# Hybrid decoder layer on one core: activation forms of the second MLP product emitted one step earlier, with other first places for banks, row tiles and split tiles

## The chip, the cores and the metric

The kernel runs on one NeuronCore of one Trainium2 chip. The metric is device microseconds of one execution. Before the change the median of three runs is 2827.7 us (2827.36 to 2830.01).

## The reference

One layer of a decoder trunk, for a prompt of 2048 rows and 8 x 8 sample rows, 2112 rows of 1024 columns in all. A token mixer (three head groups behind one input projection, one output projection) comes first, then a squared-ReLU MLP:

```
x = x + rms_norm(mix, norm_mix_post)
h = rms_norm(x, norm_mlp_pre)
f = square(relu(h @ w_mlp_up)) @ w_mlp_down      # 1024 -> 4096 -> 1024
x = x + rms_norm(f, norm_mlp_post)
```

The outputs are x for prompt and sample rows and the new caches and states. The change lies in the MLP alone. Everything is float32.

## The kernel before, in words

**Three passes for one product.** A float32 product is made of three matmuls on operands that are split into a rounded high part (`hi`) and the rest (`lo`): hi x lo, hi x hi, lo x hi (`mm3`, line 282). Splitting a tile costs one cast on ScalarE (ACT) and one subtraction on VectorE (DVE) or GpSimd (POOL). An activation tile (128x352) is split in `s_pair` (line 1608): `shi` is cast on ACT, `slo` subtracted on DVE. A weight tile (128x1024) is split in `w_split` (line 1599): `whi` on ACT, `wlo` on POOL while the first MLP product runs ("up", kind u), on DVE while the second runs ("down", kind d).

**The MLP's tiling.** The rows go in three blocks of 704, each of two halves of 352. In each block both products, up and down, are made by seven part products each (a Strassen scheme: sums and differences of operand quarters are formed, and seven products in place of eight are combined). The orders are 1, 2, 6, 7, 5, 3, 4 for up and 1, 2, 7, 4, 5, 6, 3 for down. A part product is 8 steps; a step takes one weight tile pair. So the list `steps` has 3 x 2 x 7 x 8 = 336 entries. An up step is 24 matmuls of 352 columns into two PSUM banks, each of which is evicted at once by `up_out`. A down step takes two activation tiles, j and j+1 (its two halves), with 9 matmuls of 512 columns each; three banks are filled over the 8 steps and evicted by `down_out` after the last, with 3 additions on DVE for products 1, 2, 7, 4 and 3 (for product 1 copies on ACT), 6 for product 5 and 9 for product 6.

**The forms.** The left operand of down products 7, 5, 6 and 3 is first formed from two activation tiles by one DVE operation per tile (`down_form`, line 1750); products 1, 2 and 4 take a tile as it is. `down_split` (line 1745) makes form and split of one tile; the form is tied behind the DVE instruction that was emitted last before it. The left operand of an up product is four tile pairs, split once per product by `up_split` (line 1740).

**What sets the order.** The loop over `steps` emits the program. A scheduler then orders each engine's instructions: where several could go, the one that was emitted first goes first. The engines run what stands there strictly in order. In the loop each turn emits, one after the other: the load of a weight tile four steps ahead; `w_split` of the next step's weights; near the end of an up product the split of the first two pairs of the next (line 1859); the matmuls of this step and its evictions; the other two pairs (line 1886); and last the forms and splits of the next step, where that is a down step (line 1894).

**Places.** `NSP` (line 49) is the number of buffers for split activation tiles, two per pair. `bank()` (line 1680) hands out PSUM banks in the order psS, psD, psD; its counter starts at 0 and is raised first, so the first bank comes from psD, a pool that opens when the output projection's own PSUM pool closes. Rows of a half (`Half.rows`, line 1616 on) are read back from the scratch tensor `xn_d` into three tiles before they are turned by PE transposes (`pq<-cst,xt`). For the second half they are taken in turn from two tags of a pool shared with the output projection (`XT`, line 1685: xres, x2t).

Of the kernel before, what the change touches and what calls it, by code (L numbers as in the profile page):

```python
# [45 lines left out]
NSUM = 16  # L46
SUM_US = 6.4
SUM_END = {5: "a13", 7: "a13", 6: "a2", 4: "a4"}
NSP = 12

NKEY = 1288

# [92 lines left out]
def hybrid_layer(ctx: ExitStack, tc: tile.TileContext, I, O, stage=9):  # L145
# [83 lines left out]
    def sb(name, bufs, side=None):  # L229
        return tc.tile_pool(name=name, bufs=bufs, side=side, reuse_waits="tile")  # L230
# [15 lines left out]
    def stream(gen, delay=0.0):  # L246
        streams.append([gen, PE.us + delay])
# [1321 lines left out]
    UP_ORDER, DOWN_ORDER = (1, 2, 6, 7, 5, 3, 4), (1, 2, 7, 4, 5, 6, 3)  # L1569
# [24 lines left out]
    def idle_y(at):  # L1594

        kind, _, i, _ = steps[at]
        return kind == "u" and i != UP_ORDER[0]
# [10 lines left out]
    def s_pair(src):  # L1608

        hi = s4.tile([P, HT], F32R, name="shi", tag="s")  # L1610
        lo = s4.tile([P, HT], F32R, name="slo", tag="s")
        A.copy(hi, src)  # L1612
        V.tensor_sub(lo, src, hi.bitcast(F32))
        return hi, lo
# [28 lines left out]
    halves = {}  # L1643
    up_s = {}

    def mlp_ahead():
        nonlocal e4, s4, w4, r4
        psm.close()
        e4 = p4.enter_context(sb("ev4", 2, "right"))
        s4 = p4.enter_context(sb("s4", NSP, "right"))  # L1650
        r4 = p4.enter_context(sb("r4", 8, "right"))
# [18 lines left out]
    y4 = p4.enter_context(sb("y4", 6, "left"))  # L1670
# [4 lines left out]

    V.tensor_scalar(g4[:, 512:], g4[:, 512:], -1.0, None, op0=ALU.mult)

    nbank = [0]

    def bank():  # L1680
        nbank[0] += 1
# [3 lines left out]
    XT = [(epool, "xres"), (epool, "x2t")]  # L1685
# [36 lines left out]
    def up_sums(b):  # L1722

        (q11, q12), (q21, q22) = halves[b, 0].q, halves[b, 1].q
        while len(up_s.get((b, 2), [])) < 4:
            yield 1.0
        s3 = []
        for c in range(4):
            s3.append(f4.tile([P, HT], F32, name="s3", tag="f"))
            with tc.issue_after(V.last):  # L1730
                V.tensor_sub(s3[c], q11[c], q21[c])
                V.tensor_sub(q21[c], q21[c], q22[c])
                V.tensor_sub(q11[c], q21[c], q11[c])
                V.scalar_tensor_tensor(q12[c], q12[c], -1.0, q11[c], op0=ALU.mult, op1=ALU.subtract)
            yield 3.0
        src.update({(b, 6): q11, (b, 7): s3, (b, 5): q21, (b, 3): q12, (b, 4): q22})
# [3 lines left out]
    def up_split(b, i, cs):  # L1740
        up_s.setdefault((b, i), []).extend(s_pair(src[b, i][c]) for c in cs)
# [3 lines left out]
    def down_split(b, i, j):  # L1745
        with tc.issue_after(V.last):
            a = down_form(i, j)
        down_s[b, i, j] = s_pair(a)

    def down_form(i, j):  # L1750
        x = {k[:2]: v for k, v in X.items() if k[2] == j}
        if i == 1:
            a = x[1, 1]
        elif i == 2:
            a = x[1, 2]
        elif i == 7:
            a = t4.tile([P, HT], F32, name="d3", tag="t")
            V.tensor_sub(a, x[1, 1], x[2, 1])
        elif i == 4:
            a = x[2, 2]  # L1760
        elif i == 5:
            a = x[2, 1]
            V.tensor_sub(a, a, x[2, 2])
        elif i == 6:
            a = x[1, 1]
            V.tensor_sub(a, x[2, 1], a)
        else:
            a = x[1, 2]
            V.scalar_tensor_tensor(a, a, -1.0, x[1, 1], op0=ALU.mult, op1=ALU.subtract)
        return a  # L1770

    def down_out(i, p, ps):
        n = TP[p][1]
        ps = ps[:n]

        def y(t, d, new=False):
            if new:
                Y[t, p] = y4.tile([P, D], F32, name=f"y{t}", tag="y")
            return Y[t, p][:n, 512 * (d - 1):512 * d]

        if i == 1:
            A.copy(y(1, 2, True), ps)
        elif i == 2:
            V.tensor_add(y(1, 1), ps, y(1, 2))
        elif i == 7:
            V.tensor_add(y(2, 2, True), ps, y(1, 2))
        elif i == 4:
            V.tensor_add(y(2, 1), ps, y(2, 2))
        elif i == 5:
            for d in ((2, 2), (1, 2)):  # L1790
                V.tensor_sub(y(*d), y(*d), ps)
        elif i == 6:
            for d in ((2, 1), (2, 2), (1, 2)):
                V.tensor_add(y(*d), ps, y(*d))
        else:
            V.tensor_add(y(1, 2), ps, y(1, 2))
# [28 lines left out]

    def second_half(b):

        h = halves[b, 1] = Half(b, 1, XT)
        h.rows()
        yield 10.0  # L1830
        yield from h.turn(psT, "tr")
        yield from up_sums(b)
# [12 lines left out]
    for at, (kind, b, i, jj) in enumerate(steps):  # L1845
        if at + 4 < len(steps):
            w_load(at + 4)
        while nsplit[0] < len(steps) and nsplit[0] <= at + (2 if idle_y(nsplit[0]) else 1):
            w_split(nsplit[0])
            nsplit[0] += 1  # L1850
        order = UP_ORDER if kind == "u" else DOWN_ORDER
        nxt = steps[at + 2] if at + 2 < len(steps) else None

        if kind == "u" and jj == NJ // 2 - 2 and i != UP_ORDER[-1]:
            ni = UP_ORDER[UP_ORDER.index(i) + 1]
            if ni == 6:
                while (b, 6) not in src:
                    advance(min(streams, key=lambda st: st[1]))
            up_split(b, ni, (0, 1))
        if kind == "d" and i == DOWN_ORDER[-1] and jj == NJ // 2 - 1 and (b + 1, 1) in src:  # L1860
            up_split(b + 1, 1, (0, 1))
        two = steps[at + 1] if at + 1 < len(steps) else None
        if kind == "u":
            hi, lo = wts.pop(at)
            s = up_s[b, i]
            for j2 in range(2):
                ps = bank()
                for c in range(4):
                    ws = slice(2 * P * c + P * j2, 2 * P * c + P * j2 + P)
                    mm3(ps[:, :HT], hi[:, ws], lo[:, ws], *s[c], c == 0, c == 3)  # L1870
                up_out(i, 2 * jj + j2, ps)
        else:
            hi, lo = wts.pop(at)
            if jj == 0:
                banks = [bank() for _ in TP]
            for j2 in range(2):
                j = 2 * jj + j2
                s = down_s.pop((b, i, j))
                ws = slice(512 * j2, 512 * j2 + 512)
                for p, (a, n) in enumerate(TP):  # L1880
                    mm3(banks[p][:n], s[0][:, a:a + n], s[1][:, a:a + n], hi[:, ws], lo[:, ws], j == 0, j == NJ - 1)
            if jj == NJ // 2 - 1:
                for p in range(len(TP)):
                    down_out(i, p, banks[p])
        if kind == "u" and jj == NJ // 2 - 1 and i != UP_ORDER[-1]:
            up_split(b, UP_ORDER[UP_ORDER.index(i) + 1], (2, 3))
        if kind == "d" and i == DOWN_ORDER[-1] and jj == NJ // 2 - 1 and b + 1 < TT // BT:
            while (b + 1, 1) not in src:
                advance(min(streams, key=lambda st: st[1]))
            have = len(up_s.get((b + 1, 1), []))  # L1890
            up_split(b + 1, 1, range(have, 4))
        if two is not None and two[0] == "d":
            for j2 in range(2):
                down_split(two[1], two[2], 2 * two[3] + j2)
        if kind == "d":
            end, last = jj == NJ // 2 - 1, b == TT // BT - 1
            if i == 2 and end:
                for p in range(len(TP)):
                    square(1, p, 1)
                    if last:  # L1900
                        o = Y[1, p][:TP[p][1], :512]
                        V.tensor_mul(o, o, g4[:TP[p][1], :512])
            if i == 6 and end:
                for p in range(len(TP)):
                    for d in (1, 2):
                        square(2, p, d)
            if i == 3 and not end and 1 <= jj <= len(TP):
                mlp_out(b, 2, jj - 1)
            if i == 3 and end:
                for p in range(len(TP)):  # L1910
                    square(1, p, 2)
                    mlp_out(b, 1, p, last)
        if kind == "d" and i == 6 and jj == 2 and b + 1 < TT // BT:
            stream(next_block(b + 1))
        if at % 20 == 10 and shifts:
            nm, sr, sb_ = shifts.pop(0)
            with tc.issue_after(wload[0].ins):
                SP.dma_start(O[nm][0, sb_, 0:WB - NS].rearrange("t h e -> t (h e)"),
                                  I[sr][0, sb_, NS:WB].rearrange("t h e -> t (h e)"))
        poll()  # L1920
# [38 lines left out]
```

## Time and profile before

| | us |
|---|---|
| median of three runs | 2827.7 |
| profiled execution, its own time | 2828.42 |
| its span, first to last instruction | 2826.6 |
| PE busy (matmuls) | 2595.9, 92% |
| DVE busy | 1536.4, 54% |
| ACT busy | 1325.4, 47% |
| POOL busy | 1076.7, 38% |
| mean granted TensorE clock | 0.963 |

The first matmul of the MLP (`pm`) starts 1307.5 us into the span, the last at 2809.5 us. Block 0's down products run from 1581.1 to 1836.2 us, block 1's from 2066.9 to 2324.4, block 2's from 2554.4 on. In the trace an idle time stands in brackets behind the instruction that ended it, with what released it. A weight load for matmuls (LDWEIGHTS) is listed as PEld. Where a helper records an operation, its line is the helper's: every DVE and POOL operation of the MLP stands under L137, every matmul under L118, every transpose under L122; L1604 is `whi`, L1612 `shi`, L1638 the turned rows.

### The profile page before, as it was taken

To read this page: it belongs to the slowest core of one execution; us is meant where nothing else is said; L and a number is where in the kernel's file an instruction comes from. 1 tells how busy PE (TensorE), PEld (TensorE's weight loads), DVE (VectorE), ACT (ScalarE), POOL (GpSimd) and SP (SyncE) were. 2 spreads that over 40 slices of the span, in tenths; PEclk is the share of its full clock that TensorE was granted. 3 is DMA by queue.
4 is the path that set the end of the run, shared out by engine and by line. 5 is a ranking of instruction groups with operands and counts; after the bars stand their busy time and mean duration, and the time that the engine had idled before them with its cause. 6 is when DMAs were issued, how large, how long until landed. Compare 5 with 4: busy or idle time off the path is not lost. (4 is left out here: it accounts for less than half of the span.)

```text
span 2826.6 us, 40785 instructions
## 1 busy us (share of the span) xinstructions
PE 2595.9 (92%) x14329; PEld 2194.3 (78%) x14329; DVE 1536.4 (54%) x2994; ACT 1325.4 (47%) x2776; POOL 1076.7 (38%) x1008
## 2 busy tenths in 40 slices
PE   7998889999989978999899999999999998999996
PEld 6897767877877755556899876799987678998764
DVE  4555436455446556454255466744446674445666
ACT  4534335435435333334437644453854355385433
POOL 4445445444454543334566200166610026660002
PEclk9999989999999989999999999999999999999998
DMA  7777998777677559877877445474434446544343
GB/s 207 214 185 223 270 252 230 197 215 206 178 214 205 148 165 285 264 225 245 247 227 206 127 149 162 154 220 135 164 126 147 139 143 195 169 157 134 134 127 86
DMA packets 426261, 528.27 MB, mean 187 GB/s; under 512 B 65482, under 2 KB 326130, under 8 KB 421448
## 3 DMA queue, kind: packets, MB, share of 16 engines
q1 hardware_dynamic: 411352, 483.45, 54.0%
q0 software_dynamic: 14704, 42.21, 9.0%
q8 instruction: 113, 1.85, 0.3%
q14 instruction: 92, 0.75, 0.1%
HBM read 447.90 MB, written 178.19 MB: 221 GB/s over the span
## 5 line engine op out<-in xcount | busy, mean ns | idle before, releaser
L137 POOL TENSOR_TENSOR wlo<-wraw,whi 128x512 fp32r<-128x512 f32 (+2 forms) x359 | 670.8, 1898 | 557.0 <-ACT whi L417 290.6
L1604 ACT CAST whi<-wraw 128x1024 fp32r<-128x1024 f32 x336 | 351.7, 1049 | 360.1 <-PE pm L118 300.8
L118 PE MATMUL pm<-slo,whi 128*128 128x352 f32 x1344 | 439.1, 328 | 15.0 <-DVE slo L137 5.1
L118 PE MATMUL pm<-wlo,shi 128*128 128x512 f32 (+1 forms) x1008 | 404.6, 401 | 42.5 <-ACT shi L1612 41.9
L118 PE MATMUL pm<-shi,whi 128*128 128x352 f32 x1344 | 437.4, 326 | 0.0
L118 PE MATMUL pm<-shi,wlo 128*128 128x352 f32 x1344 | 429.5, 328 | 6.2 <-POOL wlo L137 6.1
L118 PE MATMUL pm<-whi,shi 128*128 128x512 f32 (+1 forms) x1008 | 402.3, 399 | 0.0
L118 PE MATMUL pm<-whi,slo 128*128 128x512 f32 (+1 forms) x1008 | 338.3, 398 | 0.6 <-DVE slo L137 0.6
L137 DVE TENSOR_TENSOR wlo<-wraw,whi 128x1024 fp32r<-128x1024 f32 (+1 forms) x169 | 206.2, 1220 | 204.3 <-ACT whi L1604 200.1
L118 PE MATMUL pj<-lo,whi 128*128 128x512 f32 (+1 forms) x720 | 273.2, 380 | 16.8 <-ACT xr L631 8.5
L118 PEld LDWEIGHTS pm<-slo,whi 128*128 128x128 f32 x1344 | 256.0, 191 | 19.3 <-ACT whi L1604 6.3
L118 PE MATMUL pj<-hi,whi 128*128 128x512 f32 (+1 forms) x720 | 263.5, 366 | 0.0
L118 PEld LDWEIGHTS pm<-wlo,shi 128*128 128x128 f32 (+1 forms) x1008 | 183.5, 182 | 102.7 <-ACT shi L1612 48.6
L118 PE MATMUL pj<-hi,wlo 128*128 128x512 f32 (+1 forms) x720 | 262.9, 366 | 0.0
L137 POOL TENSOR_TENSOR ssf<-ssf 128x1 f32<-128x1 f32 (+1 forms) x18 | 6.7, 373 | 668.1 <-ACT jkf L1805 668.0
L118 PEld LDWEIGHTS pm<-shi,wlo 128*128 128x128 f32 x1344 | 254.8, 191 | 7.5 <-POOL wlo L137 7.4
L118 PEld LDWEIGHTS pm<-shi,whi 128*128 128x128 f32 x1344 | 256.0, 190 | 0.1
L137 DVE TENSOR_TENSOR x<-pm,x 128x352 f32<-128x352 f32 x240 | 124.2, 521 | 222.6 <-PE pm L118 222.4
L118 PEld LDWEIGHTS pm<-whi,slo 128*128 128x128 f32 (+1 forms) x1008 | 182.1, 182 | 55.3 <-DVE slo L137 2.7
L118 PEld LDWEIGHTS pm<-whi,shi 128*128 128x128 f32 (+1 forms) x1008 | 183.9, 182 | 52.6
L1612 ACT CAST shi<-x 128x352 fp32r<-128x352 f32 x288 | 136.8, 484 | 173.7 <-DVE x L137 119.1
L137 DVE TENSOR_TENSOR slo<-x,shi 128x352 fp32r<-128x352 f32 x288 | 157.0, 554 | 40.8 <-ACT shi L1612 38.6
(324 smaller groups left out, 4892.8 us busy)
## 6 DMA issues: line engine op xcount, KB each, us to landing
wraw<-in_w_in SPq DMA_DIRECT2D x192, 256.0 KB
wraw<-u_d SPq DMA_DIRECT2D x96, 512.0 KB
wraw<-d_d SPq DMA_DIRECT2D x96, 512.0 KB
wraw<-in_w_mlp_up SPq DMA_DIRECT2D x72, 512.0 KB
wraw<-in_w_mlp_down SPq DMA_DIRECT2D x72, 512.0 KB
u_d<-in_w_mlp_up POOLq DMA_DIRECT2D x64, 256.0 KB, 5.7
d_d<-in_w_mlp_down POOLq DMA_DIRECT2D x64, 256.0 KB, 7.0
out_s_k<-in_cache_attn_k SPq DMA_DIRECT2D x8, 2040.0 KB
```

Of the source, the lines that this page charges most:

```text
L118: return self.eng.matmul(out, lhsT, rhs, **kw)
L137: out = f(*args, **kw)
L1604: A.copy(hi, raw)
L1612: A.copy(hi, src)
```

## The change

Five edits, all in the MLP's driver.

- Where a down step follows a down step, its forms and splits are emitted ahead of the current step's matmuls and evictions. Where a down step follows an up step, they still come behind the matmuls.
- Three of the four pairs of the next up product are split ahead of the last step but one, and one behind the last, in place of two and two.
- `NSP` is 14 in place of 12.
- The bank counter starts at 2, so the first bank is one of psS.
- The rows of the second half of block 0 go to the pool `y4`, made for the down outputs, in place of `XT`.

```diff
-NSP = 12
+NSP = 14
...
-    nbank = [0]
+    nbank = [2]
...
-        h = halves[b, 1] = Half(b, 1, XT)
+        h = halves[b, 1] = Half(b, 1, XT if b else [(y4, "y")])
...
-            up_split(b, ni, (0, 1))
+            up_split(b, ni, (0, 1, 2))
         if kind == "d" and i == DOWN_ORDER[-1] and jj == NJ // 2 - 1 and (b + 1, 1) in src:
-            up_split(b + 1, 1, (0, 1))
+            up_split(b + 1, 1, (0, 1, 2))
+
         two = steps[at + 1] if at + 1 < len(steps) else None
+        if two is not None and two[0] == "d" and kind == "d":
+            for j2 in range(2):
+                down_split(two[1], two[2], 2 * two[3] + j2)
...
+        if two is not None and two[0] == "d" and kind == "u":
+            for j2 in range(2):
+                down_split(two[1], two[2], 2 * two[3] + j2)
         if kind == "u" and jj == NJ // 2 - 1 and i != UP_ORDER[-1]:
-            up_split(b, UP_ORDER[UP_ORDER.index(i) + 1], (2, 3))
+            up_split(b, UP_ORDER[UP_ORDER.index(i) + 1], (3,))
...
-        if two is not None and two[0] == "d":
-            for j2 in range(2):
-                down_split(two[1], two[2], 2 * two[3] + j2)
```

What this does to the engines' programs is shown at three places. Numbers behind names tell buffers apart; they differ a little between the two programs.

**DVE, from down product 6 to 3 in block 0, before.** `y1`, `y2` `<-pm` are product 6's nine evictions, `x12` the forms of product 3 (each in place), `slo` the low part of a form, `wlo4_17952` and `wlo4_18016` the low weights of product 3's first and second step:

```order
L137 TENSOR_TENSOR wlo4_17952<-wraw4_17847,whi4_17951 128x1024
L137 TENSOR_TENSOR slo_17946<-x11_14704,shi_17945 128x352
L137 TENSOR_TENSOR y2_17142<-pm_17708,y2_17142 128x512 x2
L137 TENSOR_TENSOR y1_16572<-pm_17708,y1_16572 128x512
L137 TENSOR_TENSOR y2_17144<-pm_17709,y2_17144 128x512 x2
L137 TENSOR_TENSOR y1_16574<-pm_17709,y1_16574 128x512
L137 TENSOR_TENSOR y2_17146<-pm_17710,y2_17146 96x512 x2
L137 TENSOR_TENSOR y1_16576<-pm_17710,y1_16576 96x512
L137 SCALAR_TENSOR_TENSOR x12_14005<-x12_14005,x11_14356 128x352
L137 TENSOR_TENSOR wlo4_18016<-wraw4_17881,whi4_18015 128x1024
L137 SCALAR_TENSOR_TENSOR x12_14048<-x12_14048,x11_14402 128x352
L137 TENSOR_TENSOR slo_17984<-x12_14005,shi_17983 128x352
```

The same place after the change (the form `x12_14005` stands just ahead of the first row):

```order
L137 TENSOR_TENSOR slo_17928<-x11_14708,shi_17927 128x352
L137 TENSOR_TENSOR slo_17957<-x12_14005,shi_17956 128x352
L137 SCALAR_TENSOR_TENSOR x12_14020<-x12_14020,x11_14373 128x352
L137 TENSOR_TENSOR y2_17150<-pm_17718,y2_17150 128x512 x2
L137 TENSOR_TENSOR y1_16580<-pm_17718,y1_16580 128x512
L137 TENSOR_TENSOR y2_17152<-pm_17719,y2_17152 128x512 x2
L137 TENSOR_TENSOR y1_16582<-pm_17719,y1_16582 128x512
L137 TENSOR_TENSOR y2_17154<-pm_17720,y2_17154 96x512 x2
L137 TENSOR_TENSOR y1_16584<-pm_17720,y1_16584 96x512
L137 TENSOR_TENSOR wlo4_18016<-wraw4_17881,whi4_18015 128x1024
L137 SCALAR_TENSOR_TENSOR x12_14048<-x12_14048,x11_14402 128x352
L137 TENSOR_TENSOR slo_17962<-x12_14020,shi_17961 128x352
```

The form and `slo` of the first tile and the form of the second have moved ahead of the evictions; the second tile's `slo` stands behind them, behind the next weights and behind one form more.

**DVE, in the sums that precede up product 6 in block 1, before.** `x11<-pm` are evictions, `s3` and `q` the sums of quarters; the last two `slo` are the third and the fourth pair of product 6:

```order
L137 TENSOR_TENSOR x11_19007<-pm_18994,x12_18632 128x352
L137 TENSOR_TENSOR s3_19011<-q_18150,q_18638 128x352
L137 TENSOR_TENSOR q_18638<-q_18638,q_18834 128x352
L137 TENSOR_TENSOR q_18150<-q_18638,q_18150 128x352
L137 TENSOR_TENSOR x11_19043<-pm_19030,x12_18671 128x352
L137 SCALAR_TENSOR_TENSOR q_18319<-q_18319,q_18150 128x352
L137 TENSOR_TENSOR x11_19060<-pm_19047,x12_18686 128x352
L137 TENSOR_TENSOR x11_19083<-pm_19070,x12_18713 128x352
L137 TENSOR_TENSOR slo_19105<-q_18102,shi_19104 128x352
L137 TENSOR_TENSOR slo_19109<-q_18150,shi_19108 128x352
```

After:

```order
L137 TENSOR_TENSOR slo_19031<-q_18102,shi_19030 128x352
L137 TENSOR_TENSOR x11_19007<-pm_18994,x12_18632 128x352
L137 TENSOR_TENSOR s3_19011<-q_18150,q_18638 128x352
L137 TENSOR_TENSOR q_18638<-q_18638,q_18834 128x352
L137 TENSOR_TENSOR q_18150<-q_18638,q_18150 128x352
L137 TENSOR_TENSOR x11_19047<-pm_19034,x12_18675 128x352
L137 SCALAR_TENSOR_TENSOR q_18319<-q_18319,q_18150 128x352
L137 TENSOR_TENSOR x11_19064<-pm_19051,x12_18690 128x352
L137 TENSOR_TENSOR x11_19087<-pm_19074,x12_18717 128x352
L137 TENSOR_TENSOR slo_19109<-q_18150,shi_19108 128x352
```

The third pair has moved up by eight rows; the fourth stands where it stood.

**SP, the DMA queue at the start of the MLP, before.** `xt4_14022`, `xt4_14024` and `xt4_14026` are the three row tiles of block 0's second half, `xn_d_102<-xres_13884` writes the last rows of the output projection, `xt4_17809` is a row tile of block 1:

```order
L137 DMA xn_d_102<-xres_13760 128x1024
L137 DMA xt4_14022<-xn_d_102 128x1024
L137 DMA xt4_14024<-xn_d_102 128x1024
L137 DMA gpost_10744<-in_norm_mlp_post 128x1024
L137 DMA out_y_sample<-x2t_13950 64x1024
L137 DMA xn_d_102<-xres_13884 64x1024
L137 DMA xt4_17809<-xn_d_102 128x1024
L137 DMA xt4_14026<-xn_d_102 96x1024
L137 DMA wraw4_14065<-in_w_mlp_up 128x4x256
```

After:

```order
L137 DMA xn_d_102<-xres_13760 128x1024
L137 DMA xt4_14022<-xn_d_102 128x1024
L137 DMA xt4_14024<-xn_d_102 128x1024
L137 DMA xt4_14026<-xn_d_102 96x1024
L137 DMA xt4_17807<-xn_d_102 128x1024
L137 DMA xt4_17809<-xn_d_102 128x1024
L137 DMA gpost_10744<-in_norm_mlp_post 128x1024
L137 DMA out_y_sample<-x2t_13950 64x1024
L137 DMA wraw4_14065<-in_w_mlp_up 128x4x256
```

The third row tile has moved up by five places, directly behind the second; the write of the last rows has gone below the weight load.

## The prediction

> **What bounds the kernel now.** I read the page first, then the waits of PE in the MLP, then the timeline at single waits.
>
> ```profile
> PE 2595.9 (92%) x14329; PEld 2194.3 (78%) x14329; DVE 1536.4 (54%) x2994; ACT 1325.4 (47%) x2776; POOL 1076.7 (38%) x1008
> ```
>
> PE is the bound. It does the same matmuls before and after, so only its idle time and its clock can change. The waits of PE from 1300 us to the end (total us, times, longest):
>
> ```profile
> PE pm L118 <- ACT shi L1612: 41.9, 12, 6.0
> PE pq L122 <- DMA xt<-xn_d: 7.8, 3, 6.6
> PE pm L118 <- DVE slo L137: 5.8, 4, 1.9
> PE pm L118 <- ACT whi L1604: 4.3, 8, 0.9
> PE pm L118 <- DVE x2t L137: 3.3, 1, 3.3
> ```
>
> The first row is the one to look at: twelve waits, four in each block. In block 0 they are, in windows around the starts of down products 7, 5, 6 and 3:
>
> ```profile
> PE pm L118 <- ACT shi L1612: 2.1, 1, 2.1
> PE pm L118 <- ACT shi L1612: 1.7, 1, 1.7
> PE pm L118 <- ACT shi L1612: 4.1, 1, 4.1
> PE pm L118 <- ACT shi L1612: 6.0, 1, 6.0
> ```
>
> They are the four products whose left operand is formed, and each wait follows the evictions of the product before: 3, 3, 6 and 9 DVE operations. The longest of them in the timeline (start, duration; the wait in brackets):
>
> ```profile
> 1794.47 0.85 PE L118 MATMUL pm<-whi,slo 128*128 128x512 f32 x3
> 1794.90 5.47 DVE L137 TENSOR_TENSOR y<-pm,y 128x512 f32<-128x512 f32 x9 [1.86 <-PE pm L118]
> ...
> 1800.29 0.51 DVE L137 SCALAR_TENSOR_TENSOR x<-x,x 128x352 f32<-128x352 f32 x1
> 1800.72 1.21 DVE L137 TENSOR_TENSOR wlo<-wraw,whi 128x1024 fp32r<-128x1024 f32 x1
> 1800.83 0.48 ACT L1612 CAST shi<-x 128x352 fp32r<-128x352 f32 x1
> 1801.37 0.79 PE L118 MATMUL pm<-wlo,shi 128*128 128x512 f32 x1 [6.04 <-ACT shi L1612]
> 1801.86 0.51 DVE L137 SCALAR_TENSOR_TENSOR x<-x,x 128x352 f32<-128x352 f32 x1
> ...
> 1802.39 0.63 PE L118 MATMUL pm<-wlo,shi 128*128 128x512 f32 x1
> 1802.82 0.63 PE L118 MATMUL pm<-whi,shi 128*128 128x512 f32 x1
> ...
> 1804.96 0.39 PE L118 MATMUL pm<-wlo,shi 128*128 128x512 f32 x1
> 1805.19 0.40 PE L118 MATMUL pm<-whi,shi 128*128 128x512 f32 x1
> ```
>
> Nine evictions, then the form, then `shi`, then PE. The row of ACT is only the last link; DVE's evictions are the wait. The pace is seen too: right behind the wait matmuls start 0.43 us apart, later 0.23. The granted clock says why (window, PE busy, clock):
>
> ```profile
> 1801.40:1804.40 3.00, 3.00 (x7) 0.50 0.36 102
> 1805.00:1808.00 3.00, 3.00 (x15) 1.00 0.03 10
> 1721.00:1724.00 3.00, 3.00 (x11) 1.00 0.45 93
> 2138.10:2141.10 3.00, 3.00 (x9) 0.65 0.44 156
> ```
>
> After the waits of 4 and 6 us the clock stands at half for about 3.2 us; after the 1.7 us at 1721 it doesn't, after the 2.1 us at 2138 it does. So a wait of 2 us or more costs on top 3.2 x (1 - 0.23/0.43) = 1.5 us. Of the twelve, eight are of that kind (product 7 in two blocks, 6 and 3 in all): 12.0 us.
>
> **The change part by part.** *Forms ahead.* Let zero be the moment at which PE could start the next product: behind product 6, three last matmuls from 1794.47, 0.23 apart, so 1795.16. A down step is 18 matmuls of 0.23, 4.14 us; each half needs its `shi` for six, then its `slo` for three. The first half thus needs `shi` at 0 and `slo` at 1.38, the second `shi` at 2.07 and `slo` at 3.45, the next step `shi` at 4.14. Before, all forms lay behind the evictions. Now one form, its `slo` and the second form lie ahead; the second `slo` lies behind them, behind the next `wlo`, and behind product 3 one form more.
>
> Behind product 6, evictions start at -0.26 and run 0.60 apart (1794.90 to 1800.29 for nine, 5.39): done at 5.13. `wlo` takes 1.14 until the next may start (1800.72 to 1801.86), the form 0.43 (1800.29 to 1800.72), the `slo` some 0.5: 7.2, with 0.05 to reach PE. Needed 3.45. **The wait of 6.0 becomes 3.8**, a half step later. Behind product 5, six evictions end at 3.33, `wlo` at 4.47, `slo` at 5.0: 1.6, and as the order puts the second step's `slo` behind the weights of the third, another 0.7 in that step: 4.1 becomes 2.3. Behind products 2 and 4 three evictions end by 1.5, `wlo` by 2.6, the next step's form by 3.1; its `shi` comes on ACT behind a weight cast, near 4.9, against 4.14: 2.1 and 1.7 become 0.8 each. The sum per block falls from 14.0 (41.9 / 3) to 7.7: over three blocks 41.9 - 23.1 = 18.8 us. Of the half-clock stretches the three behind 3.8 us stay; those of product 7 go, and those of product 6 too, since its 2.3 comes in two pieces of under 1.7, the size that kept the clock: 5 x 1.5 = 7.5. Together **-26.3 us**. Bounds: if everything is hidden, -41.9 - 12.0 = -53.9. If DVE operations don't overlap and squares on ACT come in between, so that each takes its full row (9 x 0.68, 1.21, 0.51, 0.51), 3.8 becomes 4.7, 2.3 becomes 3.0 and 0.8 becomes 1.3: 41.9 - 30.9 = 11, with two stretches fewer: -14.
>
> The Trainium skill ("TensorE: Matmul & The Clock Gate", Part 1, What's actually happening) says that the clock halves after at least one idle window of about 3.4 us and returns after one busy window, the window running free of the kernel. By that rule alone six waits of before (4.1 and 6.0 us in each block) would halve it, three would remain, and the sum would be 3 us smaller (2797 us); the 2.1 us wait at 2138 speaks against it here, so the row is taken.
>
> *Rows of the second half.* SP's timeline and the transposes that wait for it:
>
> ```profile
> 1345.53 0.80 SPq L137 DMA_DIRECT2D xt<-xn_d  x2
> ...
> 1356.98 0.48 SPq L137 DMA_DIRECT2D xn_d<-xres  x1
> 1357.56 2.70 SPq L137 DMA_DIRECT2D xt<-xn_d  x2
> ```
>
> ```profile
> 1352.39 0.55 PE L122 MATMUL pq<-cst,xt 128*128 128x128 f32 x3 [0.79 <-DMA xt<-xn_d]
> ...
> 1354.77 0.32 PE L118 MATMUL pm<-slo,whi 128*128 128x352 f32 x1
> 1354.93 0.32 PE L118 MATMUL pm<-shi,whi 128*128 128x352 f32 x1
> ...
> 1364.08 0.58 PE L122 MATMUL pq<-cst,xt 96*128 96x96 f32 x2 [6.58 <-DMA xt<-xn_d]
> ...
> 1364.81 0.49 PE L118 MATMUL pm<-slo,whi 128*128 128x352 f32 x1
> 1365.10 0.49 PE L118 MATMUL pm<-shi,whi 128*128 128x352 f32 x1
> ```
>
> The windows with a half clock there and at up product 6 of blocks 0 and 1:
>
> ```profile
> 1426.60:1432.40 5.80, 5.80 (x20) 0.50 0.13 37
> 1913.60:1917.00 3.40, 3.40 (x12) 0.51 0.47 154
> ...
> 1364.10:1367.60 3.50, 3.50 (x13) 0.51 0.76 265
> ```
>
> The third tile is issued 11 us after the others, behind the write at 1356.98, since its buffer is still used by the output projection. In `y4` it follows the second at once. The first two took 1345.53 to 1352.4; the third, 0.4 us behind and three quarters their size, should land 1 to 2 us later, and PE's new order asks for it early, so about 1.5 stays. The clock was at half behind this wait as well (1364.1 to 1367.6, 352-column matmuls 0.29 apart in place of 0.16, 1.6 us lost). Sum: 6.58 + 1.6 - 1.5 = **-6.7 us**. Bounds: 0, if the new buffers or SP's queue hold the loads just as long (the queue now issues two tiles of block 1 ahead of a weight load, and wherever one of them waits for its buffer all behind it wait), and -8.2.
>
> *First bank and 14 places.* The bank that exists earlier lets the first bank's 12 matmuls run among the output projection's; the second bank still waits for psD (3.3 us, row `x2t`). 12 x 0.16 = 1.9 us of work fill idle time there or push other work back: bounds -1.9 and, if the earlier weight split on POOL delays the projection's end, one `wlo`, +2.5. I take 0.
>
> *Three pairs ahead.* Only the start of up product 6 waits for its pairs, in every block: the row `DVE slo`. Block 1:
>
> ```profile
> 1910.64 0.43 PE L118 MATMUL pm<-slo,whi 128*128 128x352 f32 x1 [0.94 <-ACT whi L1604]
> ```
>
> ```profile
> 1910.66 2.38 POOL L137 TENSOR_TENSOR wlo<-wraw,whi 128x1024 fp32r<-128x1024 f32 x1 [2.89 <-ACT whi L1604]
> ```
>
> ```profile
> 1911.92 1.94 DVE L137 TENSOR_TENSOR slo<-q,shi 128x352 fp32r<-128x352 f32 x2 [2.04 <-ACT shi L1612]
> ```
>
> Two `slo` of 0.5 take 1.94 us, until POOL's operation beside them has ended at 1913.04. PE waits 1.9 for the third pair. After the change the third is ready long before, but the fourth stands where it stood, behind the same two activations, and meets the same POOL operation. PE asks for it three matmuls later: 0.48 us saved per block, **-1.4 us**. Bounds: the whole wait with the half clock behind it (up to 5.8 us from 1426.6, 3.4 from 1913.6) over three blocks, -15, and one POOL operation more in each, +7.
>
> **Sum:** -26.3 - 6.7 + 0 - 1.4 = -34.4. The profiled execution took 2828.4 us, 0.7 over the median; so **2794.0 us**.
>
> **The rivals.** *All hidden.* The first halves give DVE enough lead and no wait over 1 us stays: 2828.4 - 53.9 - 6.7 - 1.4 = 2766. For it: DVE is busy 54% in all. Against it: DVE's strict order puts the second `slo` behind nine evictions.
>
> *The wait moves.* Full rows, as in the bound above, and the rows arrive no sooner: -14 in all, 2814. For it: evictions, weights and forms are one queue, and 5 us of work must fit beside 3.45 us of matmuls.
>
> *Rows no sooner, the rest as forecast*: 2801.
>
> *Slower: up evictions behind POOL.* The third pair's `slo` now stands among evictions at each of 18 up products. If each met POOL's 2.4 us operation and PE waited for the bank behind it, 18 x 2.4 = 43 us are added: 2828 - 34 + 43 = 2837. It decides from 14 such waits on. For it: the 1.94 us above. Against it: six banks of 1.9 us each lie between an eviction and the next use of its bank. The Trainium skill ("SBUF — State Buffer", Who interferes with whom) states that a DVE tensor_tensor with both inputs in SBUF and a GpSimd operation that reads SBUF exclude each other, whichever came first keeping the port to its end. The trace agrees (1.94 for two of 0.5).
>
> **How the numbers follow.** The forecast 0.60, rows no sooner 0.10, the wait moves 0.14, all hidden 0.11, slower 0.03, no effect 0.02. Its own terms give the forecast some 10 us to either side. The range is 2777 to 2814: it leaves out the case that hides all, the slower one and the far end of the second. A difference of 0.2%, 5.7 us, can be told here; only the last two cases are not faster: 0.95 faster, 0.02 within 0.2%, 0.03 slower.
>
> **What would show it.** Right: the row `ACT shi` falls from 41.9 to under 12, new rows of `DVE slo` waits appear at the second half of the first steps of products 3 and 6, with 3 to 4 us each at product 3 and the clock at half behind them alone; the DMA row falls under 3. Wrong: waits for `slo` of over 5 us at product 3; a third row tile issued after 1350 us; PE waiting for `x` at up products; or no waits at product 3 at all.

## The result and the profile after

The changed kernel takes 2796.9 us (median of 4 runs, 2795.7 to 2804.0), where the kernel before took 2827.5 beside it (2819.5 to 2830.0). The ratio is 0.9902, with an interval of 0.9876 to 0.9927; it compares the means of the runs, which lie 27.8 us apart, where the medians lie 30.7 us apart. The forecast was 2794.0 in a range of 2777 to 2814. The profiled execution took 2796.83 us, its span is 2794.9 (before 2826.6).

The busy times on the page of the changed kernel:

```profile
PE 2588.7 (93%) x14329; PEld 2186.8 (78%) x14329; DVE 1531.4 (55%) x2994; ACT 1327.7 (48%) x2776; POOL 1078.8 (39%) x1008
```

The matmuls are as many as before and PE's busy time is 7.2 us less: that is the clock. The rest must lie in the waits of PE from 1300 us to the end (total us, times, longest), in the changed kernel:

```profile
PE pm L118 <- DVE slo L137: 27.6, 14, 3.7
PE pm L118 <- POOL wlo L137: 7.5, 3, 3.7
PE pq L122 <- DMA xt<-xn_d: 3.6, 3, 2.0
PE pm L118 <- DVE x2t L137: 3.5, 1, 3.5
PE pm L118 <- ACT whi L1604: 2.6, 5, 0.9
PE pm L118 <- ACT shi L1612: 1.7, 5, 0.4
```

The row `ACT shi` has gone from 41.9 to 1.7. In its place stands `DVE slo`, 27.6 against 5.8 before: 17.6 of it in the down parts, so some two fifths of the removed wait came back one half step later, and 10.0 at up product 6. The DMA row fell from 7.8 to 3.6.

The longest new wait, behind product 6 in block 0, in the timeline of the changed kernel:

```profile
1780.70 0.52 DVE L137 SCALAR_TENSOR_TENSOR x<-x,x 128x352 f32<-128x352 f32 x1
...
1781.47 5.47 DVE L137 TENSOR_TENSOR y<-pm,y 128x512 f32<-128x512 f32 x9 [0.25 <-PE pm L118]
...
1786.86 1.21 DVE L137 TENSOR_TENSOR wlo<-wraw,whi 128x1024 fp32r<-128x1024 f32 x1
...
1787.99 0.52 DVE L137 SCALAR_TENSOR_TENSOR x<-x,x 128x352 f32<-128x352 f32 x1
...
1788.43 0.52 DVE L137 TENSOR_TENSOR slo<-x,shi 128x352 fp32r<-128x352 f32 x1
```

```profile
1789.00 1.46 PE L118 MATMUL pm<-whi,slo 128*128 128x512 f32 x3 [3.65 <-DVE slo L137]
```

This is the queue that the prediction wrote down: one form ahead of the nine evictions, then the evictions, the next `wlo`, one more form, and only then the `slo` that PE waits for. PE stood still for 3.65 us where 3.8 were worked out. At product 6 the wait comes in two pieces in blocks 0 and 1 (here block 0), and in one of 1.89 us in block 2:

```profile
1750.62 0.97 PE L118 MATMUL pm<-whi,slo 128*128 128x512 f32 x3 [1.21 <-DVE slo L137]
1753.83 0.96 PE L118 MATMUL pm<-whi,slo 128*128 128x512 f32 x3 [0.51 <-DVE slo L137]
```

The three down parts together, as windows (us, PE busy); first the kernel before, then the changed one, each part from the first down matmul of a block to the first up matmul of the next, and in block 2 to the last matmul:

```profile
sum 767.70, PE 724.00; mean PE 241.33
```

```profile
sum 739.80, PE 719.27; mean PE 239.76
```

The down parts are 27.9 us shorter: 4.7 us less PE busy, that is faster matmuls, and 23.2 us less waiting. That is most of the change. The other two places are the start of the MLP and up product 6. Block 1's product 6 in the changed kernel:

```profile
1894.60 0.32 PE L118 MATMUL pm<-slo,whi 128*128 128x352 f32 x1
...
1895.79 2.35 POOL L137 TENSOR_TENSOR wlo<-wraw,whi 128x1024 fp32r<-128x1024 f32 x1 [3.45 <-ACT whi L1604]
...
1896.54 0.47 ACT L1612 CAST shi<-q 128x352 fp32r<-128x352 f32 x1
...
1897.04 1.48 DVE L137 TENSOR_TENSOR slo<-q,shi 128x352 fp32r<-128x352 f32 x1 [2.03 <-ACT shi L1612]
...
1898.58 0.66 PE L118 MATMUL pm<-slo,whi 128*128 128x352 f32 x1 [3.65 <-DVE slo L137]
```

Here two waits of 0.94 and 1.93 us have become one of 3.65. The third pair is early. The fourth is ready only 0.4 us behind the end of POOL's weight split, and that now starts 4.1 us behind product 6's first matmul (1895.79 against 1891.71), where it was 3.5 (1910.66 against 1907.16).

### The profile page after: what moved, and what is told of

Read it like the earlier page. It is cut to its first block, busy times and chain, and to the rows that moved or that the text cites. A ratio compares the mean times of both kernels' runs of the same rounds, so it can differ in the third digit from the quotient of the medians.

```text
span 2794.9 us, 40722 instructions
## 1 busy us (share of the span) xinstructions
PE 2588.7 (93%) x14329; PEld 2186.8 (78%) x14329; DVE 1531.4 (55%) x2994; ACT 1327.7 (48%) x2776; POOL 1078.8 (39%) x1008
## 3 DMA queue, kind: packets, MB, share of 16 engines
q8 instruction: 113, 1.85, 0.3%
## 5 line engine op out<-in xcount | busy, mean ns | idle before, releaser
L118 PE MATMUL pm<-whi,slo 128*128 128x512 f32 (+1 forms) x1008 | 338.1, 399 | 17.6 <-DVE slo L137 17.6
```

What stands on the lines that cost most here:

```text
L118: return self.eng.matmul(out, lhsT, rhs, **kw)
```

## The experiments

All ratios are to the kernel before, run beside the experiment on the same chip.

### Which edit carries the gain

`forms_alone` has the first edit alone, `rest_alone` the other four:

```diff
 # forms_alone, against before
+        if two is not None and two[0] == "d" and kind == "d":
+            for j2 in range(2):
+                down_split(two[1], two[2], 2 * two[3] + j2)
...
 # rest_alone, against before
-NSP = 12
+NSP = 14
...
-    nbank = [0]
+    nbank = [2]
...
-        h = halves[b, 1] = Half(b, 1, XT)
+        h = halves[b, 1] = Half(b, 1, XT if b else [(y4, "y")])
...
-            up_split(b, ni, (0, 1))
+            up_split(b, ni, (0, 1, 2))
...
```

> The kernel before with one edit of the five: forms and splits of the next down step emitted ahead of the current step's matmuls. Theory (the gain is DVE's evictions no longer standing ahead of the first form; between the two traces the three down stages shortened by 8.9, 8.9 and 9.8 us): 27 us less than before, near 2800 us, with waits for slo of 3 to 4 us at each product 3 and about 1.2 at product 6, and the waits for the DMA of xt<-xn_d (6.6 us) as before. Rival (the five edits need each other, since 12 places don't hold two steps' splits beside each other): under 15 us less, and waits for shi of over 2 us at products 6 and 3.

> The kernel before with the other four edits (three pairs ahead, 14 places, first bank from psS, rows in y4), forms where they were. Theory: 4 to 7 us less than before (start 6.7 less, up product 6 between 1.4 less and 3 more), about 2822 us, the row of waits for shi at 42 us as before. Rival that the row tiles come no sooner or the earlier matmuls only push other work back: no change, 2827 us. Rival that the up splits help as they were meant to: 15 us less or more.

Measured: forms_alone 2804.0 us, ratio 0.9925 (0.9908 to 0.9942); rest_alone 2821.5, ratio 0.9982 (0.9970 to 0.9993). PE's waits from 1300 us on, first in forms_alone, then in rest_alone:

```profile
PE pm L118 <- DVE slo L137: 22.0, 13, 3.6
PE pq L122 <- DMA xt<-xn_d: 6.8, 2, 6.1
```

```profile
PE pm L118 <- ACT shi L1612: 42.1, 12, 6.1
PE pm L118 <- DVE slo L137: 10.1, 4, 3.7
```

The forms carry about three quarters of the change (22.1 of 30.7 us by the medians, 0.0075 of 0.0098 by the ratios), some 5 us less than was expected of them alone. The row of waits for `shi` falls with that edit, from 41.9 to 1.8, and stays without it, and the `slo` waits at product 3 are the same 3.6 us in forms_alone.

### Is it DVE's queue that is left?

If the remaining wait is the place of the second `slo` behind the evictions, forms made two steps ahead must remove it, and the next thing in the queue, the second step's `wlo`, must be waited for. If that is right, this `wlo` on POOL, which has little to do in the down parts, must remove that as well.

```diff
 # two_steps_ahead, against the changed kernel (formed_d is filled in down_split)
-        if two is not None and two[0] == "d" and kind == "d":
-            for j2 in range(2):
-                down_split(two[1], two[2], 2 * two[3] + j2)
+        for st in (steps[at + 1:at + 3] if kind == "d" else []):
+            if st[0] == "d" and st[1] == b:
+                for j2 in range(2):
+                    if (st[1], st[2], 2 * st[3] + j2) not in formed_d:
+                        down_split(st[1], st[2], 2 * st[3] + j2)
 # two_steps_pool, against two_steps_ahead
-        (G if steps[at][0] == "u" else V).tensor_sub(lo, raw, hi.bitcast(F32))
+        (G if steps[at][0] == "u" or (steps[at][2] in (6, 3) and steps[at][3] == 1) else V).tensor_sub(lo, raw, hi.bitcast(F32))
```

> The changed kernel, with the forms and splits emitted for the next two down steps in place of one. Theory (the 3.65 us left at product 3 and the 1.2 at product 6 are the second half's slo, which DVE's order keeps behind the evictions): those waits go; what stands behind the evictions then is the second step's low weights, which are due 4.1 us after the product's start, so waits of 2 to 2.5 us for wlo appear at the second steps of products 3 and 6. 6 to 12 us less than the changed kernel, about 2788 us. Rival (the wait is ACT, whose squares of product 6's outputs lie between the casts, or PSUM): waits of 3 to 4 us at product 3's first step stay, within 3 us of the changed kernel.

> As two_steps_ahead, and the low weights of the second step of down products 6 and 3 made on POOL, which is idle in the down stages, in place of DVE. Theory: nothing that PE needs in the first two steps stands behind the evictions any more; waits at products 6 and 3 fall under 1.5 us each and the clock stays up there: 15 to 28 us less than the changed kernel, 2770 to 2782 us. Rival (POOL's 2.4 us operation holds up DVE's slo beside it, as at up product 6, and the weights come too late): the time of two_steps_ahead or more, with waits for slo or wlo of over 2 us at the second step.

Measured: two_steps_ahead 2785.3 us, 0.9864 (0.9841 to 0.9888); two_steps_pool 2763.9, 0.9780 (0.9764 to 0.9796). PE's waits in the first and in the second:

```profile
PE pm L118 <- DVE wlo L137: 16.3, 6, 4.5
PE pm L118 <- DVE slo L137: 10.0, 4, 3.6
```

```profile
PE pm L118 <- DVE slo L137: 15.7, 8, 3.7
PE pm L118 <- POOL wlo L137: 5.7, 5, 3.7
```

With both forms ahead, `slo` is no longer waited for at products 6 and 3 (the 10.0 left are up product 6), and PE stands at the second step's `wlo` in all six places, for 2.3 to 2.7 us and once for 4.5. Taking that one operation from DVE's queue removes the row `DVE wlo` and 21 us; what is left at product 3 is 1.9 us of `slo` in each block, more than the 1.5 foreseen, though the gain is larger than the 15 to 28 us foreseen. So the wait is DVE's strict order behind the evictions, as the prediction said.

### The start of the MLP

The prediction gave 6.7 us to the row tiles and nothing to the first bank. Four runs take these edits apart.

```diff
 # rows_alone, against before
-        h = halves[b, 1] = Half(b, 1, XT)
+        h = halves[b, 1] = Half(b, 1, XT if b else [(y4, "y")])
 # bank_alone, against before
-    nbank = [0]
+    nbank = [2]
 # bank_and_rows: both of these
 # change_without_rows, against the changed kernel
-        h = halves[b, 1] = Half(b, 1, XT if b else [(y4, "y")])
+        h = halves[b, 1] = Half(b, 1, XT)
```

> The kernel before with one edit: the rows of block 0's second half go to y4. Theory (the third row tile's 11 us later issue is what PE waits for): the wait of 6.6 us for xt<-xn_d becomes 1 to 2 us and the half clock behind it goes, 5 to 7 us less than before, about 2820 us, all else as before. Rival (the gain at the start seen in the changed kernel comes from the first bank or from the earlier weight loads): under 2 us less.

> Only the bank counter's start is changed (the first bank comes from psS); all else as before. Open from the runs so far: the four edits beside the forms gain 5 us together, the second half's rows in other buffers gain nothing alone (1.0009 of before) and neither do the three pairs with 14 places (0.9998). Theory BANK (the bank alone carries the gain): 5 us under the kernel before, about 2822, with the MLP 5 to 8 us shorter than the 1464 us of before. Theory JOINT (bank and rows gain only together): within 2 us of before, about 2827, with the wait of 6.6 us for the third row tile still there. Theory PREDICTION (my term of 0 for the bank, bounds -1.9 to +2.5): 2825 to 2829.

> The bank counter's start and the second half's rows in the output pool are changed together; forms, pairs and places as before. Theory JOINT: 5 us under the kernel before, about 2822, no wait over 2.5 us for a row tile, and no wait for ACT's queue of over 1 us behind it (rows alone had 1.6 and 1.2 us there). Theory BANK: also about 2822, but then bank_alone is as fast. Theory PAIRS (the gain needs the pairs and the 14 places too): no gain, about 2827. Theory CLOCK (the loss of rows alone lies in half-clock stretches that fall by chance): 2822 to 2827, with the stretches at other places in the profile.

> The whole change, with only the rows of block 0's second half put back into the old buffers. The changed kernel took 2796.9. Theory PREDICTION (the rows carry 6.7 us of the change): 2803 to 2804, with a wait of over 5 us for the third row tile. Theory BANK (seen with the bank alone: its new place also lets 72 in place of 28 matmuls run ahead of the third tile's transposes, so the late tile is covered): no loss, 2793 to 2799, the wait for the third tile 1 to 3 us, and the first down product 228 to 231 us behind the wait for x2t (228.6 in the changed kernel, 235.7 before).

| | us | ratio | interval |
|---|---|---|---|
| rows_alone | 2827.2 | 1.0009 | 0.9997 to 1.0021 |
| bank_alone | 2824.2 | 0.9983 | 0.9971 to 0.9995 |
| bank_and_rows | 2827.4 | 1.0005 | 0.9990 to 1.0020 |
| change_without_rows | 2791.3 | 0.9888 | 0.9865 to 0.9910 |
| the change | 2796.9 | 0.9902 | 0.9876 to 0.9927 |

The rows were a miss: alone they gain nothing, and the change without them is no slower. The bank alone gains 4.7 us by the medians, with an interval that leaves 1 out. In rows_alone the tile did come early; PE's waits from the wait for `x2t` (1341.2) to the first down product, and then the timeline of the same kernel at the first of the new waits:

```profile
PE pq L122 <- ACT q L1638: 2.8, 2, 1.6
PE pm L118 <- DVE x L137: 2.5, 1, 2.5
...
PE pm L118 <- ACT whi L1604: 1.3, 2, 0.9
PE pq L122 <- DMA xt<-xn_d: 0.8, 1, 0.8
```

```profile
1365.88 1.04 ACT L1604 CAST whi<-wraw 128x1024 fp32r<-128x1024 f32 x1 [4.94 <-DMA wraw<-in_w_mlp_up]
...
1367.18 0.56 ACT L1638 ACTIVATE q<-pq,vec 128x352 f32<-128x352 f32 x1
...
1367.79 0.44 PE L122 MATMUL pq<-cst,xt 128*128 128x128 f32 x2 [1.56 <-ACT q L1638]
```

The wait for the tile fell from 7.4 to 0.8. But PE then arrives sooner at the next weights, whose load is no sooner: ACT waits 4.94 us for `wraw` with its `whi` cast, the turned rows `q` stand behind that cast in ACT's order, and PE waits for `q` and for `whi`. The old wait had been cover for these loads. Together with one more stretch at half clock in this part (five of 3.4 us in place of four) it comes to nothing: from the `x2t` wait to the first down product 235.3 us against 235.6.

The same part of bank_alone as a window (us, PE busy and matmuls, clock, then the DMA engines' share and GB/s), and its waits in it:

```profile
1345.70:1574.40 228.70, 222.85 (x1348) 0.97 0.75 222
```

```profile
PE pm L118 <- DVE x2t L137: 3.5, 1, 3.5
PE pm L118 <- DVE x L137: 2.3, 2, 2.1
PE pq L122 <- DMA xt<-xn_d: 2.3, 1, 2.3
```

With the first bank from psS the scheduler gives PE another order. Before, 36 matmuls of the MLP stand between the `x2t` wait and the first transposes, and 28 between the second and the third tile's transposes. In bank_alone it is 24 and 72: twelve ran ahead of the `x2t` wait, and the third tile is turned 44 matmuls later, 7 us at 0.16. Its load is as late as before (issued at 1357.73, behind the write at 1357.16), but PE has work until it comes, and waits 2.3 us in place of 6.6. So the late tile was covered, not made early.

That window flatters the bank, since its twelve matmuls ahead of the `x2t` wait aren't in it and push the projection's end back. From a point that no edit touches, the 200th last matmul of the output projection, to the first down product the profiles have:

| | us | | us |
|---|---|---|---|
| before | 296.3 | pairs_alone (next section) | 292.4 |
| bank_alone | 292.2 | change_without_pairs (next section) | 293.4 |
| rows_alone | 295.9 | change_without_rows | 290.4 |
| bank_and_rows | 297.0 | the change | 293.0 |

The order of before took 296.3 us here and 296.9 in forms_alone, that of the changed kernel 293.0 and, in three other kernels with the same order, 291.8 to 292.2; so the start did gain. But two profiles show how far a single one can be trusted: in bank_and_rows and change_without_pairs the matmuls and transposes of this part stand in the same order, one by one, and it takes 297.0 us in one and 293.4 in the other. The first has five stretches of 3.4 us at half clock from the `x2t` wait on, the second three. So 3.6 us can come without any edit, as much as the edits seem to be worth; and pairs_alone, with neither the bank nor the rows, is as short as bank_alone in its profile and no faster than before in its median.

What is shown is that the bank alone gains and the rows alone don't. Bank and rows together gain nothing that can be measured (1.0005): there the transposes of the third tile stand early again (24 matmuls, then all three tiles), and the wait for `q` is 3.2 us in two pieces. They stand as early in the changed kernel, so what covers the late tile in bank_alone isn't at work in it. Which edits give the changed kernel the 3.3 us of its start stays open; no run takes the bank alone out of it.

### Up product 6

`pairs_alone` has the three pairs and the 14 places alone, `change_without_pairs` everything else. `u6_weights_dve` takes POOL's weight split out of the way: in the changed kernel, the two weight splits around the start of product 6 go to DVE.

```diff
 # pairs_alone, against before (undone in change_without_pairs)
-NSP = 12
+NSP = 14
...
-            up_split(b, ni, (0, 1))
+            up_split(b, ni, (0, 1, 2))
...
-            up_split(b, UP_ORDER[UP_ORDER.index(i) + 1], (2, 3))
+            up_split(b, UP_ORDER[UP_ORDER.index(i) + 1], (3,))
 # u6_weights_dve, against the changed kernel
-        (G if steps[at][0] == "u" else V).tensor_sub(lo, raw, hi.bitcast(F32))
+        (G if steps[at][0] == "u" and not ((steps[at][2], steps[at][3]) in ((2, 7), (6, 0))) else V).tensor_sub(lo, raw, hi.bitcast(F32))
```

> The kernel before with the three pairs ahead and 14 places alone. Theory (the fourth pair's slo meets POOL's weight split, whatever is done with the third): the two waits of 0.9 and 1.9 us at up product 6 of blocks 1 and 2 become one of 2.5 to 3.7 us, the clock is at half behind it as before; within 2 us of before, and if anything more. Rival (the third pair was what PE waited for): the waits at up product 6 fall under 1 us, the clock stays up, 8 to 15 us less.

> The whole change, with only the pairs (two and two again) and the 12 places put back. The changed kernel took 2796.9. Theory PREDICTION (three pairs ahead are worth 1.4 us): 2798. Theory USELESS (one wait of 3.7 us at up product 6 in place of two of 0.9 and 1.9, as seen): 2795 to 2797 from that place. Theory JOINT (bank and rows without the pairs gained nothing): up to 5 us slower, about 2802, with the first down product 232 to 234 us behind the wait for x2t and five half-clock stretches in that part in place of two.

> The changed kernel, with the low weights of two up steps, the last of product 2 and the first of product 6, made on DVE in place of POOL. Theory (DVE's slo of the fourth pair is held until POOL's operation beside it ends): without that operation the 3.65 us at up product 6 of blocks 1 and 2 and the 1.2 + 1.4 us of block 0 fall under 1 us and the half clock goes: 8 to 12 us less than the changed kernel, about 2787 us. Rival (DVE has simply too much work there, sixteen sums and the evictions): the two operations of 1.2 us more on DVE make the waits longer, 3 us more or worse.

Measured: pairs_alone 2826.5 us, 0.9998 (0.9981 to 1.0015); change_without_pairs 2793.4, 0.9894 (0.9871 to 0.9916); u6_weights_dve 2780.6, 0.9841 (0.9825 to 0.9857). PE's waits from 1300 us on in pairs_alone, and then in change_without_pairs:

```profile
PE pm L118 <- DVE slo L137: 10.6, 6, 3.6
PE pm L118 <- POOL wlo L137: 7.9, 3, 3.7
```

```profile
PE pm L118 <- DVE slo L137: 22.6, 13, 3.6
PE pm L118 <- POOL wlo L137: 6.0, 2, 3.0
```

The pairs raise the `slo` row from 5.8 to 10.6 and the longest `POOL wlo` wait, at up product 1, from 3.0 to 3.7; what they take away are the waits for `x` and `whi` in front. On the clock it is nothing to be measured, with or without the rest of the change. In u6_weights_dve the row falls as expected:

```profile
PE pm L118 <- DVE slo L137: 17.5, 10, 3.7
PE pm L118 <- POOL wlo L137: 7.3, 2, 3.7
```

17.5 are the waits at the down products, as before; at product 6 PE waits in no block, and 16 us are gained, more than the 8 to 12 expected. The `slo` of block 1's four pairs take 0.51 to 0.53 us each, where the fourth took 1.48. So the wait there is the fourth pair's `slo`, held beside POOL's operation, and not the number of pairs split ahead. The run shows the place and the partner. By what the two engines exclude each other it doesn't show; the Trainium skill ("SBUF — State Buffer", Who interferes with whom) names the shared port, and a `slo` of 0.5 us that takes 1.48 until 0.4 us behind the end of POOL's 2.35 agrees.

### Both together

`joined` is two_steps_pool with the weight splits of u6_weights_dve on DVE, and one more, of the second step of up product 1 in blocks 1 and 2:

```diff
-        (G if steps[at][0] == "u" or (steps[at][2] in (6, 3) and steps[at][3] == 1) else V).tensor_sub(lo, raw, hi.bitcast(F32))
+        (G if steps[at][0] == "u" and not ((steps[at][2], steps[at][3]) in ((2, 7), (6, 0)) or steps[at][1] > 0 and steps[at][2:] in ((1, 1),)) or (steps[at][2] in (6, 3) and steps[at][3] == 1) else V).tensor_sub(lo, raw, hi.bitcast(F32))
```

> two_steps_pool with the low weights of three up steps on DVE in place of POOL: the last of product 2, the first of product 6, and the second of product 1 in blocks 1 and 2, where POOL's queue of output transfers made PE wait 3.7 us. Theory: the waits at up product 6 and at the start of blocks 1 and 2 fall under 1 us; 12 to 18 us less than two_steps_pool, about 2750 us. Rival (DVE is the next bound): the new DVE work delays evictions and slo, as much is lost as gained, 2760 us or more.

Measured: 2755.3 us, ratio 0.9755 (0.9733 to 0.9776), the lowest of these kernels. It is faster than u6_weights_dve; against two_steps_pool the intervals overlap, so that isn't clear, and the 12 to 18 us that were expected over it were not reached. PE's waits from 1300 us on:

```profile
PE pm L118 <- POOL wlo L137: 8.5, 3, 3.5
PE pm L118 <- DVE slo L137: 6.5, 5, 1.9
```

The split moved at up product 1 didn't help: 3.5 us for `POOL wlo` are left in blocks 1 and 2. PE has run 52 matmuls of the product when it stops there, two steps of 24 and four more, so it waits for the third step's weights, not for the second's. In block 1:

```profile
1818.32 2.42 POOL L137 TENSOR_TENSOR ssf<-ssf 128x1 f32<-128x1 f32 x1 [4.00 <-ACT jkf L1808]
...
1824.43 0.94 POOL L137 TENSOR_TENSOR rstd<-rstd_ms,mhalf 96x1 f32<-96x1 f32 x1
1825.34 2.33 POOL L137 TENSOR_TENSOR wlo<-wraw,whi 128x1024 fp32r<-128x1024 f32 x1
```

```profile
1827.73 0.66 PE L118 MATMUL pm<-shi,wlo 128*128 128x352 f32 x1 [3.53 <-POOL wlo L137]
```

What stands ahead of this `wlo` on POOL are the nine small operations for the norm of the last block's outputs (`ssf`, `rstd_ms`, `rstd`), not the output transfers that the expectation named.

## Why the prediction came out right, and where it didn't

The time was 2.9 us from the forecast; the terms were less exact than that.

| | predicted | measured in the profiles |
|---|---|---|
| forms: waits | -18.8 | -23.2 |
| forms: clock | -7.5 | -4.7 |
| start: rows and first bank | -6.7 | -3.3 |
| up product 6 and what follows | -1.4 | +2.9 |
| sum | -34.4 | -28.3 |

The start is counted from the 200th last matmul of the projection, the up row by the up parts of blocks 1 and 2 (230.7 and 230.0 us before, 231.5 and 232.1 after). The span fell by 31.7; the remaining 3.4 us lie ahead of that matmul, where the matmuls of both kernels stand in the same order, or are rounding. So the small miss is in good part luck: the waits gave 4.4 us more than forecast, the clock, the start and product 6 gave 2.8, 3.4 and 4.3 less, and 3.4 came from a part that the change doesn't reach.

**Forms ahead: right, in mechanism and place.** All four waits of a block came where they were put, `slo` in the second half of the first step. At product 3 3.65 was measured for 3.8, at product 6 1.7 to 1.9 for 2.3. At products 7 and 5 it was 0.3 to 0.4 for 0.8 (0.6, for `slo`, at product 7 of block 2): there "`shi` comes on ACT behind a weight cast, near 4.9" was late by half a microsecond. The rival in which the waits move at full rows (-14) falls with this: evictions did overlap at 0.60.

**The clock: the right price, the wrong number of places.** Within the down parts' stretches at half clock PE was busy for 26.4 us at eight places before, 3.3 us each where the prediction took 3.2. After the change it is 15.8 us at four places. The 10.6 us less, at the prediction's 1 - 0.23/0.43, come to 4.9 us, near the 4.7 measured. So the price held and two other steps failed. The step "those of product 6 too, since its 2.3 comes in two pieces of under 1.7" was wrong in block 2, where one wait of 1.89 us kept its stretch (2707.4). And at product 3 of block 1 the clock stood at half for 6.8 us with 5.9 us of matmuls in it, where it had been 2.9 before. Why waits of much the same length differ so is shown in the last section.

**Rows of the second half: the term that failed.** "6.58 + 1.6 - 1.5" priced one wait as if nothing else were late behind it. The tile came early, as foreseen, and the gain went to the next load: the weights that ACT then waits 4.94 us for. The bound of 0 that stood beside it was the right value, for another reason than the one given.

**First bank: taken as 0, and alone it gains.** Alone it gives 4.7 us by the medians, beyond the bound of -1.9, though the interval (1.4 to 8.2 us) reaches inside it. The step counted the twelve matmuls and not what the scheduler does with the rest: the third tile's transposes went 44 matmuls back, so that its lateness was hidden. A comparison of the two programs' PE order at that place would have shown it. What the bank is worth in the changed kernel, with the rows moved as well, isn't shown.

**Three pairs ahead: the sign was wrong.** The step was "PE asks for it three matmuls later". PE doesn't: in its order 16 matmuls of product 6 stand ahead of the wait in both programs. Before they were twelve with the first two pairs and four of the next two banks; now they are sixteen with the first three pairs. The scheduler had already filled the gap with other work, so the third pair bought no lead, and as POOL's operation starts 0.6 us later against the product, the one wait is longer than the two.

**The rivals.** *Slower by up evictions behind POOL*: no such waits at the 18 up products; PE waits for no `x` there. *All hidden*: 23.2 of 41.9 us, not all; two_steps_pool shows what it needs. *Rows no sooner* was wrong in its wording and right in its price. Of the signs named beforehand two failed: the DMA row is 3.6 and not under 3 (2.0 and 0.6 us at the start, 1.0 for a row tile of the next block), and the clock stands at half behind product 6 of block 2 as well as at product 3.

## What to carry to other kernels

Where an in-order engine makes the operands of the next product and also clears away the last one, write down its queue in time, operation by operation, and compare each with the moment at which it is needed: this gave 3.8 for 3.65 us, and named the next two late operations. A single wait at a start is not worth its length: look for the transfer that is late right behind it before the wait is counted as gained. And where a place decides a scheduler's order, compare the order of the bounding engine at each wait, not only that of the operation that was moved. Before a few us at one place are put down to an edit, look at two profiles whose order there is the same.

## What the runs showed of the hardware

**Equal waits, another clock.** In two_steps_ahead PE waits 2.27 us until 1748.25 and 2.27 us until 1784.10, and only the second wait halves the clock. Four windows of 3.41 us (us, PE busy and matmuls, clock, DMA share and GB/s):

```profile
1744.14:1747.55 3.41, 1.84 (x9) 1.00 0.24 85
1747.55:1750.96 3.41, 2.71 (x12) 1.00 0.18 69
1781.69:1785.10 3.41, 1.14 (x5) 1.00 0.44 154
1785.10:1788.51 3.41, 3.41 (x9) 0.50 0.35 86
```

These windows are not chosen freely. In each of the fourteen profiles all stretches at half clock start on one grid of 3.413 us, within 0.01 us, and where this grid lies against the kernel's work differs from profile to profile. What counts is how long PE is idle within one window of the grid. The first wait falls on two windows, with 1.57 and 0.70 us of idle time; the second lies in one, with 2.27. From 1310 us to 40 us before the end of all profiles, of the windows at full clock with under 1.6 us of idle time none of 5575 has a half clock in the next window; with 1.9 us or more it is all of 129; between the two, 15 of 41. In a window that is already at half clock less is enough: 0.6 us or more kept it there in all of 52, under 0.6 in one of 144, which is how 6.8 us come about. So the 77 waits of 3.6 us or more all halved the clock, the 18 of 1.7 to 1.85 us never did, and for a wait between them it depends on where the grid fell. The Trainium skill ("TensorE: Matmul & The Clock Gate", Part 1, What's actually happening) has such a free-running window of about 3.4 us, which agrees; that it takes a whole idle window doesn't, as 1.9 us of idle time in a window were enough.

**The kernel's first half is not repeatable to some 12 us.** In the profiles the 200th last matmul of the output projection comes between 1278.6 us (two_steps_pool) and 1291.0 us (forms_alone), with the same matmuls in the same order in front of it. That is as much as most single edits here are worth, and the reason why an effect of 3 to 5 us was read from stages counted from a fixed point, beside the medians. Even such a stage can differ by 3.6 us in the same order, as at the start of the MLP.
